# Block products of the attention values: order of their weight loads, of the fifth product's sums and of the sums of h

## The chip, the cores and the metric

The kernel runs on one core of a Trainium2 chip. The metric is device time in microseconds (us), the median of a few runs of the same program. Beside these runs there is one profiled execution, from which every row of the trace below comes.

The engines are named as in the profile: PE is TensorE's matmuls (PEld its weight loads), DVE is VectorE, ACT is ScalarE, POOL is GpSimd, and SP is SyncE, which here only issues DMA transfers. A row that begins with SPq or names a DMA on POOL is the issue of a transfer, not its data's way.

## What is computed

A decoder block over one sequence of 1024 tokens with 1024 channels: a retention branch and a dilated attention branch side by side, a gated merge, then a squared-ReLU MLP. What matters here is the head of the block:

```python
mod = jax.nn.silu(c) @ w_ada[l] + b_ada[l]
sh1, sc1, g1, sh2, sc2, g2 = jnp.split(mod, 6, axis=-1)
h = modulate(rms_norm(x, norm1_g[l]), sh1, sc1)
...
proj = h @ w_in
...
for gi, (win, dil) in enumerate(ATT_GROUPS):
    aq, ak, av = parts[4 + 3 * gi], parts[5 + 3 * gi], parts[6 + 3 * gi]
    tab = rel_bias[:, gi * ATT_HEADS_PER_GROUP:(gi + 1) * ATT_HEADS_PER_GROUP]
    o, lse = dilated_group(heads(aq, ATT_HEADS_PER_GROUP), heads(ak, ATT_HEADS_PER_GROUP),
                           heads(av, ATT_HEADS_PER_GROUP), tab, win, dil)
```

The change touches the values `av` of the three attention groups (three times 512 columns of `w_in`), the expansion of `rel_bias` into rows of bias over the distance, and the tables for the rotation of the retention's queries and keys.

## The kernel before

All matmuls are in float32, each done as three products of a high and a low part (`mm3`, lines 197 to 205): low weight by high x, high weight by low x, high by high. A weight tile of 128 x 1024 is therefore first split: ACT copies it into a rounded high part, DVE subtracts that from the raw weight to get the low part.

**Start.** `h` is made channel tile by channel tile (eight tiles, k = 0 to 7): DVE scales x, ACT adds the shift and rounds (`hh`), DVE makes the low part (`hl`). While tiles appear, `av_first` multiplies them with the weights of the first attention group into eight PSUM banks, one for each 128 tokens (`av_k`, line 746). At its end ACT copies the eight banks to SBUF (line 767) and SP writes them to DRAM.

**The stage of the change.** The other two groups are one 1024 x 1024 product, h by a weight of two by two blocks. `av_blocks` (line 968) computes it in seven block products instead of eight, of 48 matmuls each, in the order `ABSEQ` = 11, 12, s1, s2, s3, 22, s4. A product whose name begins with s has a sum of weight blocks as its weight and, but for s4, a sum of parts of h as its x. The weight sums are:

- s1 = block 21 + block 22, s2 = s1 + block 11, s4 = s2 + block 12, all made in the same pair of buffers (`AB["s", j]`, the two halves j = 0, 1 of the 1024 rows), each by one more adding load. So s2 can be made only after s1 has been split, and s4 after s2.
- s3 = block 21 + block 11, in a buffer pair of its own.

A sum is made by the DMA: SP loads one block, then POOL issues a transfer that adds the second block to what is there (`avb_add`, lines 888 and 889). Each half is 512 KB.

The sums of h, named t1 to t4, are made by `sums_of_h` (line 837): four times one DVE operation on a 128 x 512 piece, one ACT rounding and one DVE subtraction. t1 is the x of s1, t2 of s2, t3 of s3 and t4 of the product 22. They are made in place, piece upon piece, in the order t1, t3, t2, t4.

Seven products share eight PSUM banks: product 11 opens four of them (`ava` in the profile), 12 the other four (`avb`), s1 reuses the second four (`avc`), and s2, s3, 22 are accumulated onto the first four, s4 onto those of s1. Between products `avb_post` (line 943) copies or adds a bank to SBUF by ACT (11, s1, s2, 22) or DVE (12, s3, s4). A product that goes onto a bank must wait for the copy of that bank: s3 for ACT's copy of s2 (line 951), s1 for DVE's addition of 12 (line 957).

The dictionary `work` in `av_blocks` says what the other engines are told between the quarter products: the key (i, m) is "after quarter m of product i". `avb_split(m)` splits a weight tile of the first two products, `avb_split(i, j)` half j of the weight of product i. The engines work through their queues strictly in this order.

**SP's queue.** In `av_first`, after the products with tile 4, SP is given the three rows of bias for the attention groups: for each it writes 12 x 384 values to DRAM (`browd`, line 438) and then broadcasts four of these rows over 128 partitions into another DRAM tensor (`biasd`, line 441), which the attention reads much later. Behind these stand the raw weights of the first two products (`avb_load`, tiles 0, 2, 1 and, at the end, 3) and block 21 for s1. At the end of `av_first` come the first group's values, eight writes of parts of h (`h12d`), and the tables `cs` (cosine and sine, 1 MB) and `decay`. The loads of s3 and 22, and those of the first query weights (`a_load`), are issued from `work`.

Behind the stage `queries_keys` (line 1071) does the projections of queries, keys and gates in the same block manner, with products named `qap` in the profile. The rotation there reads `cs`.

Of the kernel before, what the change touches and what calls it, by code (L numbers as in the profile page):

```python
# [134 lines left out]
def block_kernel(ctx, tc, io, stop=None, dbg=None):  # L135
    nc = tc.nc
# [190 lines left out]
    decay = right0.tile([P, H * C], F32, name="decay")  # L327
    cs = right0.tile([P, 2, S], F32, name="cossin")
# [3 lines left out]
    def x4(name, dt=F32):  # L332
        return xpool.tile([P, 1024], dt, tag="x", bufs=26, name=name)
# [4 lines left out]
    rows = [x4("rows"), onehot[1][:, 384:]]  # L338
    brow_d = [dram.tile([12, 384], F32, name=f"browd{g}") for g in range(3)]
# [42 lines left out]
    def bias_cut(t, g):  # L382

        return t[0][:, 384 * g:384 * g + 384] if g < 2 else t[1][:, :384]
# [50 lines left out]

    def bias_out(g):

        nc.sync.dma_start(brow_d[g], bias_cut(rows, g)[:12])
        for a in range(4):
            src = brow_d[g][4 * g + a:4 * g + a + 1]  # L440
            nc.sync.dma_start(bias_d[g][a], src.to_broadcast([P, 384]))
# [337 lines left out]
    def av_first(kk):  # L779

        def body(ahead, w):
            for k in (2 * kk, 2 * kk + 1):
                if k == 0:
                    for j, rb in enumerate(first["rb"]):
                        nc.scalar.copy(rb1[:, 512 * j:512 * j + 512], rb)
                if k % 2 == 0:
                    ahead(1)
                if k + 1 < NK:
                    h1_mods(k + 1)
                    h1_scale(k + 1)  # L790

                    if first["lows"]:
                        first["lows"].pop(0)()
                        h1_low(k + 1)
                        if k + 2 < NK:
                            mod1(k + 2)
                    elif k + 2 < NK:
                        mod1(k + 2, (SC1,))
                        h1_low(k + 1)
                        mod1(k + 2, (SH1,))  # L800
                    else:
                        h1_low(k + 1)
                if k in (6, 7):
                    avb_split(k - 6)
                av_k(0, k, w)
                if k == 3:
                    first["release"]()
                if k == 4:
                    for g in range(3):
                        bias_out(g)  # L810
                    avb_load(0)
                if k == 5:
                    avb_load(2)
                if k == 6:
                    avb_load(1)
                    for j in range(2):
                        avb_sum(j, "s1")
                if k == NK - 1:
                    avb_load(3)
                    for m in range(4):  # L820
                        nc.sync.dma_start(h12_d[m][:, 0], fv(hh[2 * m][:, 512:]))
                        nc.sync.dma_start(h12_d[m][:, 1], fv(hl[2 * m][:, 512:]))
                    sh = mods[:, SH1:SH1 + NK].rearrange("p (m j) -> p m j", j=2)
                    nc.vector.tensor_sub(dsh1, sh[:, :, 0], sh[:, :, 1])
                    sums_of_h("t1")
                    nc.sync.dma_start(cs, io["cossin"])
                    nc.sync.dma_start(decay, io["decay"])
        return body

    XA = {}  # L830
# [6 lines left out]
    def sums_of_h(name):  # L837

        low = None
        for m in range(4):  # L840
            k = 2 * m + 1
            e, o = xt[2 * m], xt[k]
            e0, e1, o0, o1 = e[:, :512], e[:, 512:], o[:, :512], o[:, 512:]
            sh = mods[:, SH1 + k:SH1 + k + 1]
            if name == "t1":
                r = e0
                nc.vector.tensor_sub(r, e0, e1)
            elif name == "t3":
                r = e1
                nc.vector.scalar_tensor_tensor(r, e1, dsh1[:, m:m + 1], o1, op0=ALU.add, op1=ALU.subtract)  # L850
            elif name == "t2":
                r = o1
                nc.vector.scalar_tensor_tensor(r, o1, sh, e0, op0=ALU.add, op1=ALU.add)
            else:
                r = o0
                nc.vector.scalar_tensor_tensor(r, o0, sh, o1, op0=ALU.add, op1=ALU.subtract)
            if name != "t4":
                t = x4(f"xa{name}{m}", F32R)
                XA[name, m] = t[:, :512], t[:, 512:]
            if low:  # L860
                nc.vector.tensor_sub(low[0], low[1], fv(low[2]))
            hi, lo = XA[name, m]
            nc.scalar.copy(hi, r)
            low = lo, r, hi
        nc.vector.tensor_sub(low[0], low[1], fv(low[2]))
# [10 lines left out]
    def avb_load(m):  # L876
        AB["w", m] = x4(f"abr{m}")
        nc.sync.dma_start(AB["w", m], ABW[4 + m])
# [12 lines left out]
    def avb_sum(j, n):  # L891

        if n == "s1":
            AB["s", j] = wraw.tile([P, 1024], F32, tag="raw", name=f"abs{j}")
            nc.sync.dma_start(pairs_of(AB["s", j]), avb_src("21", j))
        avb_add(pairs_of(AB["s", j]), {"s1": "22", "s2": "11", "s4": "12"}[n], j)
# [3 lines left out]
    def avb_fetch(i, j):  # L900

        n = ABSEQ[i]
        raw = AB["w", i, j] = x4(f"abr{n}{j}")
        nc.sync.dma_start(pairs_of(raw), avb_src("21" if n == "s3" else "22", j))
        if n == "s3":
            avb_add(pairs_of(raw), "11", j)

    def avb_split(m, j=None):

        n = m if j is None else 2 * m + j  # L910
        sign = 1.0 if j is None else float(VPLAN[ABSEQ[m]][1])
        if j is not None and ABSEQ[m] in ("s1", "s2", "s4"):
            raw = AB["s", j]
        else:
            raw = AB.pop(("w", m) if j is None else ("w", m, j))
        hi, lo = avb_tile(n, "h", f"abh{n}"), avb_tile(n, "l", f"abl{n}")
        nc.scalar.activation(hi, raw, AF.Copy, scale=sign)
        if sign > 0:
            nc.vector.tensor_sub(lo, raw, fv(hi))
        else:  # L920
            nc.vector.scalar_tensor_tensor(lo, raw, -1.0, fv(hi), op0=ALU.mult, op1=ALU.subtract)
        AB["o", n] = hi, lo
        if j is not None and ABSEQ[m] in ("s1", "s2"):
            avb_sum(j, {"s1": "s2", "s2": "s4"}[ABSEQ[m]])
# [42 lines left out]

    def av_blocks(ahead):

        work = {(0, 0): [lambda: avb_split(2), lambda: avb_split(3)],  # L970
                (0, 1): [lambda: sums_of_h("t3")],
                (1, 0): [lambda: avb_split(2, 0)], (1, 1): [lambda: avb_split(2, 1)],
                (1, 2): [lambda: sums_of_h("t2")],
                (2, 0): [lambda: avb_split(3, 0), lambda: avb_split(3, 1)],
                (2, 1): [lambda: sums_of_h("t4")],
                (2, 2): [lambda: avb_fetch(4, 0)], (2, 3): [lambda: avb_fetch(4, 1)],
                (3, 1): [lambda: avb_fetch(5, 0), lambda: avb_split(4, 0)],
                (3, 2): [lambda: avb_split(4, 1), lambda: a_load(0, 1)],
                (3, 3): [lambda: a_load(0, 2)],
                (4, 0): [lambda: avb_fetch(5, 1)],  # L980
                (4, 1): [lambda: avb_split(5, 0)],
                (4, 2): [lambda: avb_split(5, 1), lambda: BA.prep((0, "11"))],
                (4, 3): [lambda: BA.prep((0, "s1"))],
                (5, 0): [lambda: avb_split(6, 0)], (5, 1): [lambda: avb_split(6, 1)],
                (5, 2): [lambda: a_load(1, 1), lambda: a_load(1, 2), lambda: BA.prep((0, "s3"))],
                (5, 3): [lambda: BA.prep((0, "s2"))]}
        for i in range(len(ABSEQ)):
            for m in range(4):
                avb_mm(i, m)
                for f in work.get((i, m), ()):  # L990
                    f()
        for p in range(4):
            avb_post(len(ABSEQ) - 1, p)
# [8 lines left out]
    def a_load(q, part):  # L1002
        pair = PAIRS[q]
        src = io[{"g": "w_gate2", "a": "w_aq"}.get(pair[0]) or f"w_r{pair[1]}"]
        i = 2 * pair[1] + pair[2] if pair[0] == "a" else pair[-1]
        if q == 0 or q % 2 == 0 and part == 2:
            r = x4(f"wa{q}{part}")
        else:
            r = wraw.tile([P, 1024], F32, tag="raw", name=f"wa{q}{part}")
        nc.sync.dma_start(r, src[2 * i + part - 1])  # L1010
        BA.raw[q, part] = r
# [1555 lines left out]
```

## Time and profile before

| what | us |
| --- | --- |
| runs | 2259.48, 2256.11, 2259.6 |
| median | 2259.48 |
| the profiled execution's own time | 2258.95 |
| its span in the trace | 2257.2 |
| mean granted clock of TensorE | 0.989 of full speed |

The span is the time from the first to the last instruction in the trace. A wait in the trace is told as the idle time of an engine before an instruction, with what ended that idle time behind an arrow. In an order of time, several equal instructions in a row are merged ("x8"). A matmul's listed length is longer than its distance to the next one, since matmuls are pipelined; the distance from start to start is what counts.

### The profile page before, as it was taken

Reading aid. Unit: us, or ns where it says so; the run is one execution under the profiler, and the core shown is the slowest. Engines: PE = TensorE matmul, PEld = TensorE weight load, DVE = VectorE, ACT = ScalarE, POOL = GpSimd, SP = SyncE. Lnnn points to the kernel's source line nnn. Section 1 sums busy time; section 2 is a strip of 40 time slices with the busy share of each in tenths; the row PEclk is TensorE's granted clock in tenths of the full one; section 3 lists DMA queues with packets and bytes.
Section 4 is the critical chain, followed back from the end, with each engine's and each line's share of the span. In section 5 each row is a group of like instructions: output and inputs, shape, how many; then the busy total and the mean of one; then the engine's idle time right before and its main releaser. Section 6 shows DMA issues by size and latency. Waiting matters only on the chain.

```text
span 2257.2 us, 27110 instructions
## 1 busy us (share of the span) xinstructions
PE 2177.6 (96%) x10082; PEld 1801.3 (80%) x10082; DVE 1470.3 (65%) x2303; ACT 912.2 (40%) x1671; POOL 155.3 (7%) x176
## 2 busy tenths in 40 slices
PE   7779999999998999999999999999999999999998
PEld 5668888887887888888878788888778888788887
DVE  6636777773456788764555554576866665787855
ACT  4323322223333445454534633434454445433412
POOL 0001111100011221110000000002100000000003
PEclk9989999999999999999999999999999999999999
DMA  9757999725566565549823345645134444744322
GB/s 350 222 151 239 329 271 289 232 103 197 189 235 222 161 210 194 178 139 277 225 97 92 107 177 202 243 165 178 61 135 154 154 154 142 259 159 168 122 84 75
DMA packets 157602, 414.15 MB, mean 183 GB/s; under 512 B 27222, under 2 KB 55133, under 8 KB 153054
## 3 DMA queue, kind: packets, MB, share of 16 engines
q1 hardware_dynamic: 149598, 364.19, 46.1%
q0 software_dynamic: 7872, 48.24, 9.3%
q8 instruction: 79, 1.29, 0.2%
q14 instruction: 53, 0.43, 0.1%
HBM read 321.51 MB, written 156.13 MB: 212 GB/s over the span
## 4 chain that ended last, share of the span: by engine, by line
PE 84%; DVE 5%; DMA 4%; issue 3%; ACT 2%; SPq 1%; POOL 0%; POOLq 0%; DVEq 0%; ACTq 0%
PE qap L203 5%; PE qap L205 5%; PE qap L201 5%; PE fp L201 4%; PE fp L203 4%; PE fp L205 4%; PE rg L201 3%; PE rg L203 3%; PE rg L205 3%; PE f2a L203 2%; PE f2a L205 2%; PE f2a L201 2%; PE ak L201 2%; PE ak L203 2%; PE ak L205 2%
## 5 line engine op out<-in xcount | busy, mean ns | idle before, releaser
L201 PE MATMUL qap<-hh,qaw 128*128 128x512 f32 x216 | 84.0, 389 | 0.0
L203 PE MATMUL qap<-hl,qaw 128*128 128x512 f32 x216 | 84.0, 389 | 0.0
L205 PE MATMUL qap<-hh,qaw 128*128 128x512 f32 x216 | 84.0, 389 | 0.0
L614 POOL TENSOR_TENSOR j<-qk,j 128x512 fp32r<-128x512 f32 x32 | 43.3, 1354 | 470.0 <-ACT j L613 446.7
L2026 ACT ACTIVATE a<-a 128x512 f32<-128x512 f32 x48 | 30.3, 632 | 79.2 <-DVE a L2025 79.2
L1923 POOL TENSOR_TENSOR accnf<-accnf,sqnf 128x256 f32<-128x256 f32 (+1 forms) x18 | 16.6, 922 | 621.2 <-ACT sqnf L1922 621.2
L1380 ACT ACTIVATE P<-P,ng 128x128 f32<-128x128 f32 (+1 forms) x96 | 41.9, 438 | 38.8 <-DVE ng L1377 38.8
L258 DVE TENSOR_TENSOR fw<-w1r,fw 128x512 fp32r<-128x512 f32 x48 | 33.0, 688 | 36.3 <-ACT fw L248 36.3
L2212 ACT CAST w2h<-w2s 128x512 fp32r<-128x512 f32 x36 | 22.4, 621 | 78.6 <-DVE w2s L2250 78.6
L201 PE MATMUL fp<-h2h,fw 128*128 128x512 f32 x128 | 50.0, 391 | 0.0
L205 PE MATMUL fp<-h2h,fw 128*128 128x512 f32 x128 | 49.8, 389 | 0.0
L203 PE MATMUL fp<-h2l,fw 128*128 128x512 f32 x128 | 49.8, 389 | 0.0
L201 PE MATMUL roa<-rh,rwl 128*128 128x512 f32 x128 | 49.8, 389 | 0.0
L203 PE MATMUL roa<-rl,rwh 128*128 128x512 f32 x128 | 49.8, 389 | 0.0
L205 PE MATMUL roa<-rh,rwh 128*128 128x512 f32 x128 | 49.8, 389 | 0.0
L636 ACT COPY sm<-sT 128x128 f32<-128x128 f32 x32 | 8.5, 265 | 100.9 <-PE sT L627 100.9
L1761 DVE TENSOR_TENSOR rwl<-rwl,rwh 128x1024 fp32r<-128x1024 f32 x25 | 30.2, 1221 | 29.0 <-ACT rwh L1791 29.0
L1923 POOL TENSOR_TENSOR accn<-accn,sqn 128x512 f32<-128x512 f32 x12 | 15.6, 1296 | 478.1 <-ACT sqn L1922 478.1
L201 PEld LDWEIGHTS qap<-hh,qaw 128*128 128x128 f32 x216 | 40.5, 188 | 8.5
L203 PEld LDWEIGHTS qap<-hl,qaw 128*128 128x128 f32 x216 | 40.5, 188 | 8.4
L205 PEld LDWEIGHTS qap<-hh,qaw 128*128 128x128 f32 x216 | 40.5, 188 | 8.4
L258 DVE TENSOR_TENSOR qaw<-wa,qaw 128x512 fp32r<-128x512 f32 x54 | 37.0, 686 | 6.9 <-ACT qaw L248 6.9
(3063 smaller groups left out, 7204.3 us busy)
## 6 DMA issues: line engine op xcount, KB each, us to landing
v<-vd SPq DMA_DIRECT2D x32, 512.0 KB, 4.8
raw<-in_w_ada_dram SPq DMA_DIRECT2D x32, 512.0 KB, 5.2
w1r<-in_w_ff_dram SPq DMA_DIRECT2D x32, 512.0 KB, 4.9
vd<-vo SPq DMA_DIRECT2D x24, 512.0 KB, 4.2
yt<-y POOLq DMA_DIRECT2D x6, 2048.0 KB, 15.5
xsd<-as SPq DMA_DIRECT2D x24, 512.0 KB, 2.7
w2r<-in_w_ff2s_dram SPq DMA_DIRECT2D x24, 512.0 KB, 7.2
em<-in_w_ada_dram SPq DMA_DIRECT2D x16, 512.0 KB, 10.2
```

Of the source, the lines that this page charges most:

```text
L201: nc.tensor.matmul(o, wl, xh, start=first, stop=False, skip_group_check=skip)
L203: nc.tensor.matmul(o, wh, xl, start=False, stop=False, skip_group_check=skip)
L205: nc.tensor.matmul(o, wh, xh, start=False, stop=last, skip_group_check=skip)
L258: nc.vector.tensor_sub(t[:, 512:], src, fv(t[:, :512]))
L614: nc.gpsimd.tensor_sub(t[:, 1], src, fv(t[:, 0]))
L636: nc.scalar.copy(sm, ps[:, :C])
L1380: nc.scalar.activation(v, v, AF.Exp, bias=ng[:, blk:blk + 1], accum_out=st[:, g, blk, 2 + a:3 + a])
L1761: nc.vector.tensor_sub(lo, fv(lo), fv(hi))
L1923: (nc.vector if f == 7 else nc.gpsimd).tensor_add(G["acc", key], G["acc", key], sq)
L2026: nc.scalar.activation(o, o, AF.Relu)
L2212: nc.scalar.copy(hi, src)
```

## The change

Four things are moved; no arithmetic is added or removed.

1. The three writes of bias rows stay where they are on SP; their broadcasts (`bias_out`) move into `av_blocks`, behind quarters (0, 2), (0, 3) and (1, 0).
2. The loads of raw weights 0 and 1 stand directly behind the row writes, then the loads of both halves of s3's block 21 with POOL's adds of block 11 to them; then s1's halves with their adds, then raw weights 2 and 3. s3's halves are kept in the buffer of the table `cs` in place of two tiles of their own, and so the tables are loaded later, behind (3, 2), when s3 has been split.
3. The sums of h move: t1 from the end of `av_first` to (0, 1), t3 from (0, 1) to (0, 3), t2 from (1, 2) to (2, 0), t4 from (2, 1) to (3, 2).
4. In `work` the halves of s2 are split behind (2, 1) and (2, 2), those of s3 behind (3, 0) and (3, 1), and the loads of 22 stand behind (2, 3) and (3, 1); the first query weights behind (3, 3) and (4, 0).

```diff
     def bias_out(g):
 
-        nc.sync.dma_start(brow_d[g], bias_cut(rows, g)[:12])
         for a in range(4):
...
                 if k == 4:
                     for g in range(3):
-                        bias_out(g)
+                        nc.sync.dma_start(brow_d[g], bias_cut(rows, g)[:12])
                     avb_load(0)
-                if k == 5:
-                    avb_load(2)
-                if k == 6:
                     avb_load(1)
                     for j in range(2):
+                        avb_fetch(4, j)
+                if k == 5:
+                    for j in range(2):
                         avb_sum(j, "s1")
+                    avb_load(2)
+                    avb_load(3)
                 if k == NK - 1:
-                    avb_load(3)
...
-                    sums_of_h("t1")
-                    nc.sync.dma_start(cs, io["cossin"])
-                    nc.sync.dma_start(decay, io["decay"])
...
-        raw = AB["w", i, j] = x4(f"abr{n}{j}")
+        raw = AB["w", i, j] = cs[:, j] if n == "s3" else x4(f"abr{n}{j}")
...
+        def tables():
+            nc.sync.dma_start(cs, io["cossin"])
+            nc.sync.dma_start(decay, io["decay"])
+
         work = {(0, 0): [lambda: avb_split(2), lambda: avb_split(3)],
-                (0, 1): [lambda: sums_of_h("t3")],
-                (1, 0): [lambda: avb_split(2, 0)], (1, 1): [lambda: avb_split(2, 1)],
-                (1, 2): [lambda: sums_of_h("t2")],
-                (2, 0): [lambda: avb_split(3, 0), lambda: avb_split(3, 1)],
-                (2, 1): [lambda: sums_of_h("t4")],
-                (2, 2): [lambda: avb_fetch(4, 0)], (2, 3): [lambda: avb_fetch(4, 1)],
-                (3, 1): [lambda: avb_fetch(5, 0), lambda: avb_split(4, 0)],
-                (3, 2): [lambda: avb_split(4, 1), lambda: a_load(0, 1)],
-                (3, 3): [lambda: a_load(0, 2)],
-                (4, 0): [lambda: avb_fetch(5, 1)],
+                (0, 1): [lambda: sums_of_h("t1")], (0, 2): [lambda: bias_out(0)],
+                (0, 3): [lambda: sums_of_h("t3"), lambda: bias_out(1)],
+                (1, 0): [lambda: avb_split(2, 0), lambda: bias_out(2)], (1, 1): [lambda: avb_split(2, 1)],
+                (2, 0): [lambda: sums_of_h("t2")],
+                (2, 1): [lambda: avb_split(3, 0)], (2, 2): [lambda: avb_split(3, 1)],
+                (2, 3): [lambda: avb_fetch(5, 0)],
+                (3, 0): [lambda: avb_split(4, 0)],
+                (3, 1): [lambda: avb_split(4, 1), lambda: avb_fetch(5, 1)],
+                (3, 2): [lambda: sums_of_h("t4"), tables],
+                (3, 3): [lambda: a_load(0, 1)],
+                (4, 0): [lambda: a_load(0, 2)],
                 (4, 1): [lambda: avb_split(5, 0)],
```

## The prediction

> **What bounds the kernel now.** I read the page's busy times first, then busy time by stretches cut at the stage's edges, then TensorE's waits up to 300 us, then each engine's order of time from 35 to 185 us. The page:
>
> ```profile
> span 2257.2 us, 27110 instructions
> PE 2177.6 (96%) x10082; PEld 1801.3 (80%) x10082; DVE 1470.3 (65%) x2303; ACT 912.2 (40%) x1671; POOL 155.3 (7%) x176
> ```
>
> TensorE (PE) sets the time; only where it pauses can an edit of loads and of order gain. The stretches (length, then busy time of PE, PEld, DVE, ACT, POOL, then granted clock, DMA share, GB/s):
>
> ```profile
> 72.30:180.82 108.52, 83.82 (x338) 67.01 (x337) 48.22 (x64) 39.02 (x60) 9.93 (x8) 0.89 0.63 183
> 180.82:340.00 159.18, 159.18 (x704) 131.82 (x703) 118.55 (x190) 50.17 (x86) 20.33 (x29) 1.00 0.94 293
> ```
>
> The first stretch is the stage of the change, the block products of the attention values: 24.7 us of it idle, clock 0.89. Behind it PE never pauses. In order of time (start, length, engine, line, operation, then the idle time before and what ended it):
>
> ```profile
> 70.48 1.98 PE L761 MATMUL av<-raw_528h,hl 128*128 128x512 f32 x8
> 78.47 0.80 PE L201 MATMUL ava<-abh,hl 128*128 128x512 f32 x1 [6.01 <-ACT avo L767]
> ...
> 109.54 0.66 PE L201 MATMUL avc<-abh,xat 128*128 128x512 f32 x1 [3.11 <-DVE abr L957]
> ...
> 113.26 0.39 PE L201 MATMUL avc<-abh,xat 128*128 128x512 f32 x1
> ...
> 145.79 0.80 PE L201 MATMUL ava<-abh,xat 128*128 128x512 f32 x1 [12.62 <-ACT abr L951]
> ...
> 150.88 0.40 PE L201 MATMUL ava<-abh,xat 128*128 128x512 f32 x1
> ...
> 169.94 0.39 PE L201 MATMUL avc<-abh,hl 128*128 128x512 f32 x1
> ...
> 180.82 0.39 PE L201 MATMUL qap<-hh,qaw 128*128 128x512 f32 x1
> ```
>
> The last product runs from 169.94 to 180.82: 48 matmuls in 10.88 us, 0.227 each. The stage could start at 70.48 + 8 x 0.227 = 72.30, and seven products need 7 x 10.88 = 76.16. It takes 108.52, so it loses 32.36. The waits:
>
> ```profile
> PE ava L201 <- ACT abr L951: 12.6, 1, 12.6
> ...
> PE ava L201 <- ACT avo L767: 6.0, 1, 6.0
> ...
> PE avc L201 <- DVE abr L957: 3.1, 1, 3.1
> ...
> PE ava L203 <- DVE abl L919: 1.5, 2, 0.8
> PE ava L201 <- ACT abh L917: 1.4, 2, 0.9
> ```
>
> These are 24.6 us. The other 7.8 are mostly slow matmuls after a pause: from 145.79 to 150.88 twelve take 5.09 where 2.72 would do (2.4 lost), from 109.54 to 113.26 nine take 3.72 (1.7 lost).
>
> The releasers named are only the last links. For the 6.0 us and the four short waits, the queue of SyncE (SP) shows the cause:
>
> ```profile
> 42.04 0.32 SPq L438 DMA_DIRECT2D browd<-rows  x1
> 52.27 2.49 SPq L441 DMA_DIRECT2D biasd<-browd  x4
> ...
> 67.23 1.86 SPq L878 DMA_DIRECT2D abr<-in_w_av_dram  x3
> 69.14 1.55 SPq L895 DMA_DIRECT2D abs<-in_w_av_dram  x2
> ```
>
> The broadcast of a bias row waits 10.2 us for that row's write, and the weights stand behind it until 67.23. ScalarE (ACT) then waits for them ahead of the eight copies that free the PSUM banks:
>
> ```profile
> 65.38 1.15 ACT L473 ACTIVATE hh<-xt,mods 128x1024 fp32r<-128x1024 f32 x1 [4.14 <-DVE xt L471]
> 74.30 1.06 ACT L917 ACTIVATE abh<-abr 128x1024 fp32r<-128x1024 f32 x1 [7.78 <-DMA abr<-in_w_av_dram]
> ...
> 77.85 3.99 ACT L767 COPY avo<-av 128x512 f32<-128x512 f32 x8
> ```
>
> For the 12.6 us it is GpSimd's (POOL) queue of adding loads, with the landing times of the transfers into the buffers of s1, s2 and s4 under it:
>
> ```profile
> 78.76 1.38 POOL L889 DMA_DIRECT2D abs<-in_w_av_dram  x1 [59.58 <-DMA abs<-in_w_av_dram]
> 87.14 1.24 POOL L889 DMA_DIRECT2D abs<-in_w_av_dram  x1 [7.00 <-DMA abs<-in_w_av_dram]
> ...
> 132.03 1.21 POOL L889 DMA_DIRECT2D abrs<-in_w_av_dram  x1 [5.14 <-issue]
> 138.19 1.22 POOL L889 DMA_DIRECT2D abrs<-in_w_av_dram  x1 [4.94 <-issue]
> ```
> ```profile
> DMA to landing us min/median/max: 5.9/7.2/10.7
> ```
>
> No add starts before the one ahead has landed: 6.2 us apart at best, 8.4 beside the first writes. The two of s3, which the fifth product needs, stand last, behind those of s4, which the seventh needs:
>
> ```profile
> 144.21 1.06 ACT L917 ACTIVATE abh<-abrs 128x1024 fp32r<-128x1024 f32 x1 [5.20 <-DMA abrs<-in_w_av_dram]
> 145.17 2.03 ACT L951 COPY abr<-ava 128x512 f32<-128x512 f32 x4
> ```
>
> The split of the second half stands on ACT ahead of the copies (0.5 us apart) that let the fifth product write its banks.
>
> **The change, part by part.** *Weights ahead of the broadcasts.* In the built order of instructions each SP transfer waits for the one eight places ahead of it; at 42 us that is eight in 10.2 us, 1.3 apiece. Behind the three row writes, which wait for nothing new, come two abr, the two s3 halves, two abs, two abr, all before the broadcasts. The same ten-microsecond queue that held the row puts the first abr's landing near 55. ACT, free at 66.5, splits both (1.06 each, done 68.6) before the first bank is complete (70.9), and copies from 70.9 to 74.9. The first product needs the first copy at 72.30: met. The third weight is split by 76.0 on ACT and 1.23 later on DVE, 77.2, and is needed at 72.30 + 5.44 = 77.7; the fourth by 78.3, needed at 80.5. So the 6.0 and the four short waits go. No load of the products before is passed, since those were all sent ahead of 42.04.
>
> *s3's sums first.* POOL's adds begin when the first s3 half lands. Of the five loads sent from 67.23 the fourth was there at 78.76, 2.9 us apiece at worst; with 52.3 for the queue ahead, the third load behind it gives 61.0 at worst, and 56 where loads follow each other at 1.3 (an estimate). I take 57, nearer to that, because nothing but loads is in the queue. Four adds at the median 7.2 end at 85.8, so s1's halves are there before ACT turns to them (below).
>
> *Sums of h one product later.* These rows carry their price on VectorE (DVE), and the two splits and the banks' adds that stand behind them:
>
> ```profile
> 92.62 1.41 DVE L850 SCALAR_TENSOR_TENSOR xt<-xt,dsh,xt 128x512 f32<-128x512 f32 x2
> ...
> 97.37 0.69 DVE L865 TENSOR_TENSOR xat<-xt,xat 128x512 fp32r<-128x512 f32 x1
> ...
> 100.27 1.22 DVE L919 TENSOR_TENSOR abl<-abs,abh 128x1024 fp32r<-128x1024 f32 x1 [2.21 <-ACT abh L917]
> ...
> 108.71 2.48 DVE L957 TENSOR_TENSOR abr<-abr,avb 128x512 f32<-128x512 f32 x4
> ```
>
> One set of sums is 5.44 us. In the changed order DVE does t1 and t3 from 78.3 to 89.2. ACT, done with their casts at 88.6, copies the first product (2.03), then splits s1's halves, to 92.8; DVE follows to 94.0 and adds the first bank by 94.7. The third product, due at 72.30 + 2 x 10.88 = 94.06, starts 0.6 late instead of 3.1, the rest of its adds keeping ahead at 0.6 apiece. The next products are due at 105.6 and 116.5. t2 follows on DVE to 102, in time.
>
> *The new order's own wait.* s2's adds can start when the first s1 half is split on DVE, 92.8. Two at 7.2 land at 107.2; split on ACT 108.3, on DVE 109.5; the fourth product needs this half at 105.6 + 5.44 = 111.0: met. Behind it on ACT stand the four copies of s1 (110.3) and two splits of s3 (112.4; DVE 113.6), and only then t4, which the change has put between them and the copies that open the fifth product. t4 runs to 119.1 on DVE, its last cast to 118.4 on ACT, the first copy to 119.0. The fifth product, due at 116.5, is 2.5 late. With adds at 6.2 it is 0.5 late; at 8.4, 4.1 late plus 0.9 ahead of it. The slow start behind a pause costs 1.7 in the row with 3.11, and nothing visible behind those under 1; 2.5 is nearer to 3.11, so I take 1.7. [...]
>
> *Broadcasts, tables, the 22 loads.* The twelve broadcasts follow the h writes on SP, with only the values' writes and the 22 loads behind them, needed some 20 us later. The tables wait on SP for the split of s3 (113.6), and the first query weights stand behind them: due on DVE near 125, used by PE at 148.5 + the delays. Cover over ten microseconds; without it, one to one. Nothing else is added: halves of s3 come into the table's buffer instead of their own.
>
> Sum: 32.36 - 0.6 - 2.5 - 1.7 = 27.6 gained. The profiled execution took 2258.95, 1.75 over its span, and 0.5 under the median of the runs shown; 2258.95 - 27.6 = 2231.4. Bounds: with nothing left, 2226.6; with the first add at 61 and adds at 8.4, s1's second half lands at 94.6 and s2's at 111.4, the copy comes 11.8 later at 123.2 against 115.8, and two slow starts: 10.8 left, 2237.4.
>
> **The rivals.** *The adds are slow.* They now run beside SP's loads, the bank writes, the h writes and the broadcasts. For it: a landing of 10.7. Against it: median 7.2. At 10.7 each from 57, s2's second half lands at 121.2, the copy at 133.0, 17.2 late; with three slow starts 22.3 are left: 2248.9. [...]
>
> *The other side: the adds decide all.* The same queue of six adds gives a loss against before once each takes over 12.4 us: 57 + 6 x 12.4 + 11.8 - 115.8 + 5.1 = 32.5. For it, loads of this size have been that slow under a full queue:
>
> ```profile
> wa<-in_w_rk_dram SPq DMA_DIRECT2D x2, 512.0 KB, 14.7
> ```
>
> At 14.7 it is 46.3 left: 2272.9. Against it: nothing that went into these buffers reached 12.4.
>
> *The loads don't come forward.* If the first weights still land after ACT wants them, 6.0 and a slow start of 1.7 stay: 2239.1. For it: the ten-microsecond queue at 42; against it: 25 us between sending and need.
>
> *The DMA takes it back.* Behind the stage the DMA share is 0.94. Both stretches together hold 0.63 x 108.52 + 0.94 x 159.18 = 218 us of transfers in 267.7. If they could be no denser than that, the time would stay at 2259. Against it: 27.6 less leaves 240.1, a share of 0.91, which the second stretch exceeds today; and the loads there are sent by PE's progress, so they come earlier with it.
>
> **How the numbers follow.** Forecast 0.80 (its own range 2226.6 to 2237.4); slow adds 0.08; adds over 12.4, 0.04; loads not forward 0.05; DMA takes it back 0.03. The range reaches to the case at 2239.1 and 1.5 beyond on both sides for the spread of the runs: 2225 to 2241, leaving out 0.15. Under 0.2% (4.5 us) this kernel's measurement can't tell from no change: faster 0.93, same 0.03, slower 0.04.
>
> **What would show it.** Right: the first ava matmul at 72.3 without a pause or slow start; POOL's first add between 56 and 61 and eight adds done by about 125; the first qap matmul near 153 instead of 180.82; and from there the same spacing to the end. A wait of the fifth product for ACT's copy, 0.5 to 4 us, shows t4 in its way. Wrong: waits for adds at the third or fourth product, a pause in the queries' products, or waits of ACT for abr.

## The result, and the profile after

| | before | after |
| --- | --- | --- |
| median of the runs compared | 2257.8 (4 runs, 2253.04 to 2259.6) | 2236.25 (4 runs, 2233.53 to 2240.82) |
| profiled execution | 2258.95 | 2236.08 |
| its span | 2257.2 | 2234.3 |

The ratio is 0.991, with a 95% interval of 0.9886 to 0.9933. The medians lie 21.6 us apart, the profiled executions 22.9. The prediction was 2231.4 with a range of 2225 to 2241: the time is in it, and 5 us above the forecast.

Busy time of the changed kernel's engines, from its page:

```profile
PE 2173.9 (97%) x10082; PEld 1799.7 (81%) x10082; DVE 1469.6 (66%) x2303; ACT 912.2 (41%) x1671; POOL 155.1 (7%) x176
```

The work is the same. Busy time by stretches (length, PE, PEld, DVE, ACT, POOL, granted clock, DMA share, GB/s), the first from the stage's possible start to the first query matmul:

```profile
72.50:158.75 86.25, 80.07 (x337) 64.99 (x336) 45.44 (x61) 35.44 (x56) 6.33 (x6) 0.96 0.71 202
158.75:318.00 159.25, 159.25 (x704) 131.90 (x703) 118.50 (x190) 50.21 (x86) 19.76 (x28) 1.00 0.92 290
```

The stage has shrunk from 108.52 to 86.25, and the stretch behind it, 159.25 for the same 704 matmuls, is as long as it was (159.18). From the first query matmul to the end of the span it is 2234.3 - 158.8 = 2075.5, before 2257.2 - 180.8 = 2076.4. So the gain was made in the stage and handed on whole. Seven products need 76.16; the stage loses 86.25 - 76.16 = 10.1 in place of 32.4.

TensorE's waits inside the stage, as the list of waits up to 300 us gives them (total, times, longest):

```profile
PE ava L201 <- ACT abr L948: 3.6, 1, 3.6
...
PE ava L201 <- ACT abh L914: 1.8, 1, 1.8
PE ava L203 <- DVE abl L918: 0.8, 1, 0.8
```

The 12.6, the 6.0, the 3.1 and the first product's short waits are gone; three others, 6.2 together, are there. Where they lie, in TensorE's order of time:

```profile
70.68 1.98 PE L760 MATMUL av<-raw_528h,hl 128*128 128x512 f32 x8
72.49 0.39 PE L201 MATMUL ava<-abh,hl 128*128 128x512 f32 x1
...
94.29 0.47 PE L201 MATMUL avc<-abh,xat 128*128 128x512 f32 x1
...
112.70 0.51 PE L201 MATMUL ava<-abh,xat 128*128 128x512 f32 x1 [1.81 <-ACT abh L914]
113.96 0.50 PE L203 MATMUL ava<-abl,xat 128*128 128x512 f32 x1 [0.76 <-DVE abl L918]
...
123.10 0.80 PE L201 MATMUL ava<-abh,xat 128*128 128x512 f32 x1 [3.61 <-ACT abr L948]
...
129.51 0.39 PE L201 MATMUL ava<-abh,xat 128*128 128x512 f32 x1
...
158.77 0.39 PE L201 MATMUL qap<-hh,qaw 128*128 128x512 f32 x1
```

The first product follows the last `av` matmul at once (70.68 + 8 x 0.227 = 72.49). The third starts at 94.29 where 94.25 was possible. Then come two pauses at the second half of s2's weight and one at the start of the fifth product, and behind that fifteen matmuls take 129.51 - 123.10 = 6.41 where 3.40 would do: 3.0 lost to the slow clock (in the trace, TensorE's granted clock is 0.50 from 122.48 to 129.31).

The releasers are ACT and DVE, but as before POOL's queue of adding loads tells the cause:

```profile
56.38 1.38 POOL L886 DMA_DIRECT2D cossin<-in_w_av_dram  x1 [36.98 <-DMA cossin<-in_w_av_dram]
65.36 1.23 POOL L886 DMA_DIRECT2D cossin<-in_w_av_dram  x1 [7.60 <-issue]
71.52 1.21 POOL L886 DMA_DIRECT2D abs<-in_w_av_dram  x1 [4.93 <-issue]
...
92.83 1.21 POOL L886 DMA_DIRECT2D abs<-in_w_av_dram  x1 [12.09 <-DVE abl L916]
102.98 1.22 POOL L886 DMA_DIRECT2D abs<-in_w_av_dram  x1 [8.93 <-DMA abs<-in_w_av_dram]
111.83 1.21 POOL L886 DMA_DIRECT2D abs<-in_w_av_dram  x1 [7.63 <-DMA abs<-in_w_av_dram]
```

`cossin` is the table's buffer, in which s3's halves now lie: its adds come first, 22 us earlier than any add before. The pair at 92.83 and 102.98 is s2's: 102.98 - 92.83 = 10.2 us for its first half, 111.83 - 102.98 = 8.9 for the second. SP's queue shows what ran beside them, the twelve broadcasts and, behind four writes of values, the two loads for the product 22:

```profile
86.64 9.57 SPq L440 DMA_DIRECT2D biasd<-browd  x12
96.31 2.12 SPq L963 DMA_DIRECT2D vad<-abr  x4
100.40 2.96 SPq L901 DMA_DIRECT2D abr<-in_w_av_dram  x2
```

And ACT's order shows how the late second half reaches the fifth product:

```profile
66.63 2.00 ACT L914 ACTIVATE abh<-abr 128x1024 fp32r<-128x1024 f32 x2
71.11 4.01 ACT L766 COPY avo<-av 128x512 f32<-128x512 f32 x8 [2.48 <-PE av L760]
...
111.59 1.06 ACT L914 ACTIVATE abh<-abs 128x1024 fp32r<-128x1024 f32 x1 [7.79 <-DMA abs<-in_w_av_dram]
112.56 2.04 ACT L951 ACTIVATE abr<-avc 128x512 f32<-128x512 f32 x4
114.46 2.03 ACT L914 ACTIVATE abh<-cossin 128x1024 fp32r<-128x1024 f32 x2
118.63 1.28 ACT L860 CAST hh<-xt 128x512 fp32r<-128x512 f32 x2 [2.14 <-DVE xt L853]
...
122.47 2.04 ACT L948 COPY abr<-ava 128x512 f32<-128x512 f32 x4
```

The first two weights are split at 66.63, while TensorE still multiplies, and the copies follow as soon as the banks are complete. Down the queue from 111.59 everything stands in its fixed order: s2's split, four copies of s1, the splits of s3, the casts of t4 (118.63 and on), and only then the copies at 122.47 that free the fifth product's banks.

### The profile page after: what moved, and what is told of

It reads as the page before. It is cut to its first block, busy times and chain, and to the rows that moved or that the text cites. A ratio compares the mean times of both kernels' runs of the same rounds, so it can differ in the third digit from the quotient of the medians.

```text
span 2234.3 us, 27105 instructions
## 1 busy us (share of the span) xinstructions
PE 2173.9 (97%) x10082; PEld 1799.7 (81%) x10082; DVE 1469.6 (66%) x2303; ACT 912.2 (41%) x1671; POOL 155.1 (7%) x176
## 4 chain that ended last, share of the span: by engine, by line
PE 86%; DVE 5%; ACT 2%; issue 1%; DMA 1%; POOL 0%; POOLq 0%; SPq 0%; DVEq 0%; ACTq 0%
PE qap L203 5%; PE qap L205 5%; PE qap L201 5%; PE fp L201 4%; PE fp L203 4%; PE fp L205 4%; PE rg L201 3%; PE rg L203 3%; PE rg L205 3%; PE f2a L203 2%; PE f2a L205 2%; PE f2a L201 2%; PE ak L201 2%; PE ak L203 2%; PE ak L205 2%; PE va L203 1%
## 6 DMA issues: line engine op xcount, KB each, us to landing
em<-in_w_ada_dram SPq DMA_DIRECT2D x16, 512.0 KB, 10.2
```

## The experiments

The theory after the result: the 10.1 us left are one chain, s2's two adds slowed by other transfers, and behind them t4, which the change put ahead of the copies that the fifth product needs. The rivals say that one of the moved pieces (s3 first, weights ahead, later sums of h) does nothing or harms, or that the adds are slow by themselves. Since times behind the stage differ from one execution to the next by a few us with nothing edited there (from the first query matmul to the end of the span 2074.6 with t4 late, 2078.4 with 22's loads late), the stage is read from the trace: from the end of the last `av` product to the first `qap` matmul, less 76.16. Each ratio is against runs of the kernel before on the same chip (medians 2257.97 for the first four experiments, 2257.8 for the others).

| kernel | first `ava` | first `qap` | stage's loss | median of runs | runs from, to | ratio to before, interval |
| --- | --- | --- | --- | --- | --- | --- |
| before | 78.47 | 180.82 | 32.4 | 2257.8 | 2253.04, 2259.6 | |
| after | 72.49 | 158.77 | 10.1 | 2236.25 | 2233.53, 2240.82 | 0.991, 0.9886 to 0.9933 |
| broadcasts late | 72.31 | 155.90 | 7.4 | 2235.04 | 2232.53, 2243.74 | 0.9905, 0.9881 to 0.9928 |
| t4 late | 72.20 | 152.87 | 4.5 | 2230.24 | 2228.47, 2231.55 | 0.9877, 0.9861 to 0.9894 |
| both | 72.91 | 150.57 | 1.5 | 2231.05 | 2230.13, 2236.1 | 0.9885, 0.987 to 0.9899 |
| sums at old places | 72.41 | 158.21 | 9.6 | 2234.21 | 2231.35, 2236.96 | 0.9894, 0.9879 to 0.9909 |
| 22's loads late | 73.43 | 157.80 | 8.2 | 2231.13 | 2229.1, 2237.99 | 0.9881, 0.9856 to 0.9907 |
| s3 first, nothing else | 79.42 | 175.71 | 27.3 | 2251.32 | 2248.96, 2256.43 | 0.997, 0.9956 to 0.9983 |
| all but s3 first | 72.14 | 181.09 | 32.8 | 2262.92 | 2260.89, 2266.48 | 1.002, 1.0008 to 1.0031 |
| all three late | 72.32 | 149.25 | 0.8 | 2226.96 | 2224.88, 2229.79 | 0.9858, 0.9838 to 0.9878 |

### The broadcasts away from s2's adds

```diff
-                (0, 1): [lambda: sums_of_h("t1")], (0, 2): [lambda: bias_out(0)],
-                (0, 3): [lambda: sums_of_h("t3"), lambda: bias_out(1)],
-                (1, 0): [lambda: avb_split(2, 0), lambda: bias_out(2)], (1, 1): [lambda: avb_split(2, 1)],
+                (0, 1): [lambda: sums_of_h("t1")],
+                (0, 3): [lambda: sums_of_h("t3")],
+                (1, 0): [lambda: avb_split(2, 0)], (1, 1): [lambda: avb_split(2, 1)],
...
-                (5, 3): [lambda: BA.prep((0, "s2"))]}
+                (5, 3): [lambda: BA.prep((0, "s2")), lambda: bias_out(0)],
+                (6, 0): [lambda: bias_out(1)], (6, 1): [lambda: bias_out(2)]}
```

> The changed kernel, with the twelve broadcasts of the bias rows moved from behind quarters (0, 2), (0, 3) and (1, 0) to behind (5, 3), (6, 0) and (6, 1). Theory A, the broadcasts slow s2's two adds: the two come down from 10.2 and 8.9 us to 6 to 7 each, the waits at the second half of s2 (1.8 and 0.8 us) go, the fifth product's wait falls from 3.6 to under 1.5 us, and the slow matmuls behind it shrink: 4 to 8 us faster than the changed kernel, near 2230. Rival B, the h writes or the loads of block 22 slow them, or adds take that long here whatever runs beside: the adds stay at 9 to 10 us, the waits and the time stay, near 2236.

POOL's adds in this kernel:

```profile
92.66 1.21 POOL L886 DMA_DIRECT2D abs<-in_w_av_dram  x1 [10.94 <-DVE abl L916]
99.05 1.22 POOL L886 DMA_DIRECT2D abs<-in_w_av_dram  x1 [5.17 <-DMA abs<-in_w_av_dram]
108.96 1.21 POOL L886 DMA_DIRECT2D abs<-in_w_av_dram  x1 [8.69 <-DMA abs<-in_w_av_dram]
```

Without the broadcasts the first add takes 6.4, with them 10.2; the second stays slow at 9.9. So the broadcasts account for the first half alone. The waits of 1.8 and 0.8 at s2's second half fall to 0.2, the 3.6 at the fifth product stays, and the stage loses 2.7 less. The median hardly moves, though. The profiled execution, which took 2243.74 where the other three took 2232.53 to 2237.32, shows that the new place can cost the queries. There DVE waits for the next query weights, which stand behind the last eight broadcasts on SP:

```profile
181.17 0.69 DVE L243 TENSOR_TENSOR qas<-wa 128x512 f32<-128x512 f32 x1 [4.52 <-DMA wa<-in_w_rk_dram]
```

and TensorE pauses 3.6 for it. SP issued that load at 164.82, 8.9 after the first query matmul, in the changed kernel at 162.58, 3.8 after it. How much of this the other three paid isn't shown. A transfer that nobody needs for hundreds of microseconds still needs a place where nothing stands behind or beside it.

### t4 behind the copies

```diff
-                (3, 2): [lambda: sums_of_h("t4"), tables],
+                (3, 2): [tables],
...
-                (4, 0): [lambda: a_load(0, 2)],
+                (4, 0): [lambda: sums_of_h("t4"), lambda: a_load(0, 2)],
```

> The changed kernel, with the sums t4 moved from behind (3, 2) to behind (4, 0), so that ACT's copies of product s2 stand ahead of t4's casts. Theory A, t4 turns the late add into the fifth product's wait: that wait falls from 3.6 us to under 0.5, the slow matmuls behind it go, the waits of 1.8 and 0.8 us at s2's second half stay: 5 to 7 us faster than the changed kernel, near 2230. Rival B, the late add alone sets the copies' time, through the splits of s3 on ACT: the wait falls by less than 1 us and the time stays within 2 us of 2236.

The longest waits in the stage (the next, 0.5, is for a split):

```profile
PE ava L203 <- DVE abl L918: 1.4, 2, 0.8
PE ava L201 <- DVE abr L956: 1.4, 1, 1.4
```

The 1.4 for `abr` is the sixth product's: DVE's additions stand behind its preparation of the first query weights, for which it waited 2.4 us. The fifth product no longer waits, though s2's adds are as slow as in the changed kernel (the two take 18.6 together; 19.0 there). With the 3.6 goes the slow start behind it. The first query matmul comes 5.9 earlier, and the median is 6.0 lower. So it was t4 that turned the adds' lateness into most of the loss.

### Both

> Both of the edits above in one kernel: broadcasts behind (5, 3) to (6, 1) and t4 behind (4, 0). Theory A for both: no wait of PE over 1 us between the first block product and the queries, the first query matmul near 149.5 us instead of 158.8, the time 8 to 10 us under the changed kernel, near 2227. If only one of the two counts: near 2230. If neither: 2236.

The stage went as expected (1.5 lost, first query matmul at 150.57), the time didn't: 2231.05 is no better than with t4 alone. A wait of 1.4 in the queries, at the same line as above, took a part; the rest lies in the scatter behind the stage, and wasn't traced further.

### The sums of h at their old places

```diff
+                    sums_of_h("t1")
...
-                (0, 1): [lambda: sums_of_h("t1")], (0, 2): [lambda: bias_out(0)],
-                (0, 3): [lambda: sums_of_h("t3"), lambda: bias_out(1)],
+                (0, 1): [lambda: sums_of_h("t3")], (0, 2): [lambda: bias_out(0)],
+                (0, 3): [lambda: bias_out(1)],
...
-                (2, 0): [lambda: sums_of_h("t2")],
-                (2, 1): [lambda: avb_split(3, 0)], (2, 2): [lambda: avb_split(3, 1)],
+                (1, 2): [lambda: sums_of_h("t2")],
+                (2, 1): [lambda: avb_split(3, 0), lambda: sums_of_h("t4")], (2, 2): [lambda: avb_split(3, 1)],
...
-                (3, 2): [lambda: sums_of_h("t4"), tables],
+                (3, 2): [tables],
```

> The changed kernel with all four sums of h where they were before (t1 at the end of the first group's products, t3 behind (0, 1), t2 behind (1, 2), t4 behind (2, 1)). Theory A, the move of the sums trades one wait for another: a wait of about 3 us comes back at the third weight of the first product and one of 3 to 5 at the start of the third product, but the waits for s2's second half and of the fifth product go, since PE arrives later and t4 is out of the way: within 3 us of the changed kernel, 2233 to 2239. Rival B, the move itself saved the 3.1 us and its slow start: 5 us slower or more, over 2241.

The longest wait of this kernel's stage, and below it TensorE's order at the first product, with the two others:

```profile
PE avc L201 <- DVE abr L955: 3.1, 1, 3.1
```
```profile
79.73 0.49 PE L201 MATMUL ava<-abh,hl 128*128 128x512 f32 x1 [1.73 <-ACT abh L915]
80.99 0.50 PE L203 MATMUL ava<-abl,hh 128*128 128x512 f32 x1 [0.76 <-DVE abl L917]
...
82.03 0.63 PE L205 MATMUL ava<-abh,hh 128*128 128x512 f32 x1
...
85.44 0.40 PE L203 MATMUL ava<-abl,hh 128*128 128x512 f32 x1
```

The loss is about the same in size (9.6) and elsewhere: the third weight of the first product and the 3.1 us for the banks of s1 are back, as the prediction's working of that step would have it, while s2 and the fifth product, reached later, no longer wait. Moving the sums took those waits away and, with t4, made new ones; in this kernel the move is worth nothing.

### The loads of 22 away from s2's second add

```diff
-                (2, 3): [lambda: avb_fetch(5, 0)],
...
-                (3, 1): [lambda: avb_split(4, 1), lambda: avb_fetch(5, 1)],
-                (3, 2): [lambda: sums_of_h("t4"), tables],
+                (3, 1): [lambda: avb_split(4, 1)],
+                (3, 2): [lambda: sums_of_h("t4"), tables, lambda: avb_fetch(5, 0), lambda: avb_fetch(5, 1)],
```

> The changed kernel, with the two loads of block 22 moved on SP behind the tables, which wait for the split of s3; the broadcasts and t4 stay. Theory A, the loads of 22 slow the second of s2's adds, as the broadcasts slow the first: the second add comes down from 8.9 us to about 6.3, the first stays at 10, the waits of 1.8 and 0.8 us at s2's second half go, the fifth product's wait stays at 3 to 4 us since t4 is still in its way: 2 to 4 us faster than the changed kernel, near 2233. Rival B, the second add is slow for another reason: it stays at 8.5 or more, and the time at 2236.

POOL's adds for s2 and the first for s4:

```profile
93.78 1.21 POOL L886 DMA_DIRECT2D abs<-in_w_av_dram  x1 [11.18 <-DVE abl L916]
104.44 1.22 POOL L886 DMA_DIRECT2D abs<-in_w_av_dram  x1 [9.45 <-DMA abs<-in_w_av_dram]
111.26 1.21 POOL L886 DMA_DIRECT2D abs<-in_w_av_dram  x1 [5.60 <-DMA abs<-in_w_av_dram]
```

The mirror of the first experiment: beside the broadcasts the first add takes 10.7, and without 22's loads the second takes 6.8 in place of 8.9. The 1.8 is gone, the 0.8 and the fifth product's 3.6 stay. The median is 5.1 under the changed kernel's, of which the stage shows 1.9; where the rest comes from wasn't traced.

### s3 first, and nothing else (from the kernel before)

```diff
+                        avb_fetch(4, j)
+                    for j in range(2):
                         avb_sum(j, "s1")
...
-                    nc.sync.dma_start(cs, io["cossin"])
-                    nc.sync.dma_start(decay, io["decay"])
...
-                (2, 2): [lambda: avb_fetch(4, 0)], (2, 3): [lambda: avb_fetch(4, 1)],
...
-                (3, 2): [lambda: avb_split(4, 1), lambda: a_load(0, 1)],
+                (3, 2): [lambda: avb_split(4, 1), tables, lambda: a_load(0, 1)],
```

> The kernel before, with s3's loads and adds ahead of those of s1 and the tables behind s3's split; the weights stay behind the broadcasts and the sums of h where they were. Theory A, the order of the adds pays only with the weights ahead: the wait of 12.6 us before the fifth product goes, but s1's sums now end near 108 us, and the third product, whose banks stand behind their splits and t2 on DVE, waits some 10 us instead of 3.1; the 6.0 us at the start stays: 5 to 9 us faster than before, 2249 to 2253. Rival B, the parts add up: 12.6 us and its slow start of 2.4 are gained, 2243.

The longest waits of its stage, and of POOL's adds the first for s3 and the first for s1:

```profile
PE avc L201 <- DVE abr L957: 8.2, 1, 8.2
PE ava L201 <- ACT avo L767: 7.0, 1, 7.0
```
```profile
79.41 1.38 POOL L889 DMA_DIRECT2D cossin<-in_w_av_dram  x1 [60.25 <-DMA cossin<-in_w_av_dram]
...
98.41 1.21 POOL L889 DMA_DIRECT2D abs<-in_w_av_dram  x1 [8.81 <-DVE xt L850]
```

The 12.6 of the fifth product is gone. But the broadcasts still hold the weights back (7.0), so the first add starts at 79.41, and s3's two adds push those of s1 to 98.41, 20 us later than before: the third product waits 8.2 in place of 3.1. The stage's loss falls by 5.1 only.

### All but s3 first (from the changed kernel)

```diff
-                    for j in range(2):
-                        avb_fetch(4, j)
...
-        raw = AB["w", i, j] = cs[:, j] if n == "s3" else x4(f"abr{n}{j}")
+        raw = AB["w", i, j] = x4(f"abr{n}{j}")
...
-                (2, 1): [lambda: avb_split(3, 0)], (2, 2): [lambda: avb_split(3, 1)],
-                (2, 3): [lambda: avb_fetch(5, 0)],
+                (2, 1): [lambda: avb_split(3, 0)], (2, 2): [lambda: avb_split(3, 1), lambda: avb_fetch(4, 0)],
+                (2, 3): [lambda: avb_fetch(4, 1), lambda: avb_fetch(5, 0)],
```

> The changed kernel, with s3's loads and adds back where they were, behind those of s4 (in two tiles of their own). Theory A: s3's second add lands near 137 us, and with the split and t4 ahead of the copies the fifth product starts near 142.5 instead of 123.1, a wait of some 22 us: 17 to 21 us slower than the changed kernel, 2253 to 2257. Rival B, only the add's landing counts: the 12.6 us wait of before and its slow start come back, less what PE is earlier: 12 to 15 us slower, 2248 to 2251.

One long wait is left, and it is nearly all of the loss; under it are POOL's adds for s3, and on ACT the split of s3's second half and the copies that the fifth product needs:

```profile
PE ava L201 <- ACT abr L946: 28.4, 1, 28.4
```
```profile
125.80 1.21 POOL L884 DMA_DIRECT2D abrs<-in_w_av_dram  x1 [5.03 <-issue]
132.14 1.22 POOL L884 DMA_DIRECT2D abrs<-in_w_av_dram  x1 [5.12 <-issue]
...
138.49 1.06 ACT L912 ACTIVATE abh<-abrs 128x1024 fp32r<-128x1024 f32 x1 [5.52 <-DMA abrs<-in_w_av_dram]
...
145.32 2.04 ACT L946 COPY abr<-ava 128x512 f32<-128x512 f32 x4
```

The first product starts as early as in the changed kernel, and everything gained up to the fifth is spent in front of it. The fifth starts at 145.95, where the kernel before had 145.79. s3's last add begins 6.1 earlier than there (132.14 for 138.19), but t4's casts now stand on ACT between the split and the copies: these come 6.8 behind that split, in the kernel before 1.0 behind it (144.21 and 145.17). So t4 takes back here what the adds had gained. The start is 3.5 later than worked out: 1.5 because the last add was there at 138.5 in place of 137, the rest between there and the copies. The kernel is slower than the one before, by more than the stage shows: a wait far behind it, in the retention, is 3.3 in the kernels before and after and 7.9 here; why was not traced.

So the parts don't add. In the stage s3 first gives 5.1, the rest without it -0.4, both together 22.3: each takes away one of two waits in a row, and what is left grows by most or all of what was gained (8.2 for 3.1 above, 28.4 for 12.6 here, with t4's part in it).

### All three late

t4 and the loads of 22 as above, and the broadcasts of one row at a time in the queries, behind the first product of three late blocks (SP issues them from 419.6 to 458.7):

```diff
+            if n == "11" and NA - 4 <= q < NA - 1:
+                bias_out(q - NA + 4)
```

> The changed kernel with t4 behind (4, 0), the loads of 22 behind the tables, and the broadcasts behind the first product of three of the last queries (q = 13 to 15), where the DMA share is near 0.4. Theory A: both of s2's adds take 6 to 7 us, no wait over 1 us in the stage, the first query matmul near 149.5, no new wait behind it: 8 to 10 us faster than the changed kernel, near 2227, and under the version with only t4 moved (2230). Rival B, with t4 out of the way the adds' time no longer matters: within 1.5 us of 2230.

POOL's adds of s2, and the one wait in the stage:

```profile
92.66 1.21 POOL L886 DMA_DIRECT2D abs<-in_w_av_dram  x1 [11.12 <-DVE abl L916]
98.97 1.22 POOL L886 DMA_DIRECT2D abs<-in_w_av_dram  x1 [5.10 <-DMA abs<-in_w_av_dram]
104.99 1.21 POOL L886 DMA_DIRECT2D abs<-in_w_av_dram  x1 [4.79 <-DMA abs<-in_w_av_dram]
```
```profile
PE ava L201 <- DVE abr L956: 0.3, 1, 0.3
```

With neither the broadcasts nor the loads of 22 beside them the two adds take 6.3 and 6.0. The stage loses 0.8, its first query matmul comes at 149.25, and no wait appears in the queries that the changed kernel doesn't have. At 2226.96 this version beats the one before by 1.4% and the changed one by 9.3 us, with intervals that don't meet.

## Why the prediction was right, and where it was off

What the stage loses, by the prediction's terms:

| term | predicted | measured |
| --- | --- | --- |
| start of the stage, first two products' weights | 0 | 0 |
| third product | 0.6 | 0.1 |
| second half of s2's weight | 0 | 3.1 |
| fifth product behind t4 | 2.5 | 3.8 |
| slow start behind it | 1.7 | 3.0 |
| sum | 4.8 | 10.0 |

(Measured: from one matmul's start to the next, less the usual 0.227; so a pause of 1.81 counts 1.97. The stretches give 10.1.)

- **Weights ahead.** Right. ACT splits the first two at 66.63, worked out as 66.5; no pause is left up to the third product.
- **s3's sums first.** Right. The first add is at 56.38 (57 taken), and nothing waits for s3. Without this step the change loses time, as the seventh experiment shows; it is the step on which the others depend, and the prediction, which added up the gains, didn't say so. That experiment has t4 at its new place, too, and t4's part in its loss isn't taken apart.
- **Sums of h later.** Right for the third product: DVE and ACT run half a microsecond ahead of the working. But as a step of its own it gains nothing, since t4 gives back what the others save.
- **s2's adds: the step that failed.** The two adds "at 7.2 land at 107.2": they started right (92.83 against 92.8), but the second half was there only at 111.6; even the bound of 8.4 each gives 109.6 from there. In its sum the prediction costed the moved broadcasts only by what stands behind them on SP; that adds run beside them it said under a rival alone, in which every add takes 10.7. What they slow is POOL's transfers: 10.2 with them, 6.4 without. The loads of 22, moved to (2, 3), do the same to the second add: 8.9 and 9.9 with them, 6.8 and 6.0 without. Why an add takes longer beside other transfers was not shown. And unlike in that rival, not all adds were slow: apart from s2's two, s3's first took 9.0 and s1's first 8.0 (71.52 to 79.51), and nothing waited for those. One of the prediction's own signs of being wrong did appear, waits for adds at the fourth product, and the first query matmul came at 158.77 in place of 153.
- **The fifth product.** The mechanism is right: t4 between the split and the copies, confirmed by the second experiment. The copy is 122.47 + 0.5 = 123.0 in place of 119.0, about as much later as the add. TensorE itself came 2.8 later (119.3 for 116.5), so the wait grew from 2.5 to 3.6 only.
- **Slow start.** 3.0 for 1.7. The term came from the row with 3.11, where 3.4 us at a clock of 0.50 (109.66 to 113.07) lay behind the restart; here 6.2 us of it did (123.10 to 129.31), though the pauses are 3.11 and 3.61 (more of this below).
- **DMA takes it back, loads not forward.** Both fell: the stretch behind the stage kept its length at a DMA share of 0.92, and the first pause is gone.

The two mis-sized terms, 3.1 at s2 and 2.6 more at the fifth product with its slow start, less 0.5 at the third, are the 5.2 us of difference. With them removed (all three late), the time is 2226.96, where the prediction gave 2226.6 for nothing left. That the time lies in the forecast's own range, up to 2237.4, is in part luck: its upper bound had a late first add (61) and 8.4 for every add, and what came was an early first add and two over 8.4.

## What to carry to other kernels

Cost a moved transfer twice: by what waits behind it in its queue, and by which other transfers run in the time it moves to, above all a serial chain such as these adds, where each delay was handed on whole (the first add took 10.2 beside the broadcasts and 6.4 without, and the second began at 102.98 in place of 99.05). Where two waits lie in a row on one path, test the edits together: each alone gained little or lost (5.1 and -0.4 us in the stage), and the pair gained 22 us. And when an input may be late, look what stands behind it in an engine's queue (ACT's from 111.59 on, here): work that nobody awaits (t4) belongs behind the copies that free a bank, whatever its place in the order of the products.

## What the runs showed of the hardware that was not expected

**The slow clock did not follow the length of the pause.** A pause of 28.39 us was followed by 2.5 us lost to slow matmuls (all but s3 first: twelve from 145.95 to 151.14, 5.19 for 2.72), one of 3.61 by 3.0 (the changed kernel), the 3.11 of the kernel before and of the sums at old places by 1.7 each. And a pair of short pauses did it in one kernel: 1.73 and 0.76 us (the rows of the sums at old places above) were followed by eight matmuls 0.43 apart, from 82.03 to 85.44, while 1.81 and 0.76 in the changed kernel were followed by none.

The granted clock of the changed kernel, in three stretches of 3.41 us from its trace (the columns as above, TensorE's busy time first, the clock before the last two numbers):

```profile
119.07:122.48 3.41, 0.42 (x2) 0.00 (x0) 3.38 (x6) 1.96 (x5) 0.32 (x1) 1.00 0.85 295
122.48:125.89 3.41, 2.79 (x7) 2.23 (x8) 1.12 (x3) 2.98 (x6) 0.00 (x0) 0.50 1.03 286
125.89:129.31 3.42, 3.42 (x10) 2.68 (x9) 0.83 (x1) 0.00 (x0) 0.00 (x0) 0.50 0.88 244
```

In the first of them TensorE was idle for 3.0 us at a clock of 1.00; then 0.50 was granted for 6.83 us, and 1.00 again from 129.31. In the stage of the kernel before, 0.50 was granted three times: from 75.53 to 82.36 (6.83 us), from 109.66 to 113.07 (3.41) and from 136.97 to 150.62 (13.65). There 3.1 us idle, from 106.25 to 109.66, went ahead of a clock of 0.50, and 1.5 us idle, from 89.18 to 92.59, ahead of 1.00. The 1.81 and the 0.76 of the changed kernel make 1.4 us idle from 108.83 to 112.24 and 1.2 from 112.24 to 115.66; the clock was 1.00 there and on to 122.48. Why the pair of the sums at old places had slow matmuls behind it and this one had none, the runs do not show.

What these pauses cost at the slow clock was half of what was left of the stretch at 0.50 when TensorE restarted: (129.31 - 123.10) / 2 = 3.1 behind 3.61, (150.62 - 145.79) / 2 = 2.4 behind 12.62, and (113.07 - 109.66) / 2 = 1.7 behind 3.11.

**The first add of all took 9.0 us when it was s3's.** From 56.38 to 65.36 in the changed kernel, and 8.9 to 9.0 in the six experiments that start like it, as in the one where it came 23 us later (s3 first, nothing else: 79.41 to 88.37); the second took 6.2. Started with s1 (all but s3 first) it took 56.86 to 63.30, 6.4, and in the kernel before, at 78.76, 8.4. It cost nothing here, and its cause wasn't tried.
